# Turning the differential branch's probabilities with block transposes and DRAM

## The chip, the core and the metric

The kernel runs on one core of one Trainium2 chip. The metric is the device time of one execution in microseconds (us), as the median of a few runs. The engines are named as the profile names them: PE (TensorE, matrix products and transposes by an identity), PEld (its weight loads), DVE (VectorE), ACT (ScalarE), POOL (GpSimd) and SP (SyncE, which here only issues transfers). Each engine works through its own list of instructions in the order in which they were written down when the program was built; an instruction that has to wait holds up all that stand behind it on its engine.

## The reference

One transformer layer over 256 latent tokens and 256 context tokens, width 2048, all in float32. What bears on the change is the differential attention (branch b):

```python
def diff_attn(q, k, v, lam, lam_init, subln_g):
    b, n, h, _, dh = q.shape
    s = jnp.einsum('bnhid,bmhid->bhinm', q, k).astype(jnp.float32) * (dh ** -0.5)
    p = jax.nn.softmax(s, axis=-1)
    a = (p[:, :, 0] - lam * p[:, :, 1]).astype(v.dtype)
    o = jnp.einsum('bhnm,bmhe->bnhe', a, v)
    o = rms_norm(o, subln_g) * (1 - lam_init)
    return o.reshape(b, n, h * B_V_DIM)
```

There are 8 heads with two score maps each (head width 64, value width 128), 256 queries and 512 keys. Around it stand one large input projection, a second attention branch a (16 query heads, 4 key heads, plain softmax), two branch projections with sigmoid gates, an output projection, and a SwiGLU feed-forward part (2048 to 5632 and back).

## The kernel before

**Products.** A float32 product is made of three products of a rounded high part and a low rest (`mm3`, lines 233 to 235). A weight tile of 256 rows by 512 columns (512 KB, `wraw`) is loaded by a transfer that SP issues (L216); ACT casts its high part (`whi`, L227), DVE subtracts to get the low part (`wlo`, L229), and PE then does 12 matmuls of 128 x 512 with it. There are 7 buffers for raw weights, shared with `wada` tiles of another weight matrix that DVE sums up on the side (L431), and 3 each for `whi` and `wlo`. This stream of weights runs through the whole kernel.

**Branch b.** It is worked in 16 units (numbered 0 to 15 here), each one head and 128 queries. `front` (from L719) does the scores on PE (`s`, L740, 6 matmuls into the two `s` buffers that exist), the two softmaxes (row maximum on DVE L686, exponential on ACT L689, reciprocal L690), scales the second map (ACT L746) and combines both on DVE into one tile `p` of 128 queries by 512 keys (L747). `back` (from L752) is a generator that is resumed step by step between other pieces of work: it turns `p` with four PE transposes into a PSUM tile (`ptp`, L764), copies that to SBUF with ACT (`pT`, L770, 2 buffers), multiplies with the values (`o`, L785), takes squares on ACT (`junk_o`, L788), a power on POOL (`rstdo`, L120), scales on DVE (`on`, L790), and turns the small result with one more PE transpose (`otp`, L794).

**What sets the order.** A loop over 32 units (16 of branch b, then 16 of branch a) does `front` of a unit, resumes the older `back` generators with `on()`, and between them takes pieces of projections (`filler`, 12 big matmuls with one weight tile each) to spread the attention work evenly over the projection work. A scheduler in the language then orders each engine's list from its own estimate of when things are ready. So a change in one unit's steps also moves other instructions, on every engine.

**A turn by DRAM that is already there.** In the feed-forward part `turned` (L1038) turns a 128 x 512 tile otherwise: DVE transposes it in 32 x 32 blocks (L1041), POOL's queue writes it to DRAM (L1044), and four transfers on the same queue read it back so that the blocks change places (L1047).

## Time and profile before

| | us |
|---|---|
| median of 3 runs | 1711.54 (1708.84 to 1712.44) |
| the profiled execution | 1710.46 |
| its span in the trace | 1708.7 |
| PE busy in the span | 1682.3 |
| DVE busy | 1148.3 |
| ACT busy | 769.8 |
| POOL busy | 202.2 |
| branch b's units in the trace | about 380 to 620 |

A row of a group reads: line, engine, operation, output<-inputs, shape, count | busy us in all, mean ns of one | idle time of the engine just before them, and what ended it. A row of the timeline reads: start in us from the span's start, duration, engine, line, operation, count, and in brackets the idle time before it with what ended that. A row of a table of windows reads: window, its length, busy time of PE, PEld, DVE, ACT and POOL with counts, the granted PE clock (1.00 is full), the share of the transfer engines' time and GB/s.

### The profile page before, as it was taken

The page shows a single profiled execution, that of the slowest core. Times are in us where ns is not written, and L with a number is a line of the kernel's source. Part 1 is how long each engine was busy: PE and PEld are TensorE (multiplying, and loading weights), DVE is VectorE, ACT ScalarE, POOL GpSimd, SP SyncE. Part 2 cuts the span into 40 slices and gives each one's busy share as a digit, 9 for nine tenths or more (in the row PEclk, how much of TensorE's full clock was granted, in tenths as well). Part 3 has the DMA queues.
Part 4 walks back from the last instruction along what each step waited for, and adds up shares of the span by engine and source line. Part 5 has one row for each costly group of instructions (what it writes and reads, how often), then busy time and mean ns, then how long its engine had stood idle before and what let it go on. Part 6 is the DMA issues. An engine that isn't in the chain of part 4 may idle for free.

```text
span 1708.7 us, 21517 instructions
## 1 busy us (share of the span) xinstructions
PE 1682.3 (98%) x7889; PEld 1354.0 (79%) x7889; DVE 1148.3 (67%) x1459; ACT 769.8 (45%) x1045; POOL 202.2 (12%) x296
## 2 busy tenths in 40 slices
PE   6999999999999999999999999999999999999999
PEld 4676778887887778887888788888888888888887
DVE  5764779788788878996666755566666666554554
ACT  4222223246656556577544544444444444433332
POOL 1200002011031110001111101111111111100000
PEclk9999999999999999999999999999999999999999
DMA  7887785678757668676787857788888888765662
GB/s 285 304 295 267 265 333 175 210 259 259 251 179 220 223 224 282 231 246 206 244 272 237 295 173 222 222 271 264 266 270 265 266 275 255 237 219 191 219 205 91
DMA packets 181291, 413.15 MB, mean 242 GB/s; under 512 B 15008, under 2 KB 16240, under 8 KB 180928
## 3 DMA queue, kind: packets, MB, share of 16 engines
q1 hardware_dynamic: 168912, 374.23, 66.9%
q0 software_dynamic: 12272, 37.53, 7.2%
q8 instruction: 62, 1.02, 0.2%
q14 instruction: 45, 0.37, 0.1%
HBM read 395.42 MB, written 16.29 MB: 241 GB/s over the span
## 4 chain that ended last, share of the span: by engine, by line
PE 87%; DVE 5%; DMA 3%; ACT 2%; issue 2%; POOL 1%; SPq 0%; ACTq 0%; DVEq 0%; POOLq 0%
PE mm L233 26%; PE mm L234 26%; PE mm L235 26%; PE ada L290 2%; DVE wlo L229 1%; PE ptp L764 1%; ACT whi L227 1%; DMA wraw<-in_w_in_dram 1%; PE o L785 1%; PE s L740 1%; ACT p L689 1%; DMA fturn<-turn_d 0%; DMA tok<-in_x_dram 0%; DVE nr L479 0%; DMA gate_d<-gate 0%
## 5 line engine op out<-in xcount | busy, mean ns | idle before, releaser
L229 DVE TENSOR_TENSOR wlo<-wraw,whi 128x1024 fp32r<-128x1024 f32 x497 | 606.6, 1222 | 420.2 <-ACT whi L227 419.3
L227 ACT CAST whi<-wraw 128x1024 fp32r<-128x1024 f32 x498 | 523.0, 1051 | 729.1 <-PE mm L235 606.3
L234 PE MATMUL mm<-wlo,hT 128*128 128x512 f32 x684 | 266.2, 389 | 0.8 <-DVE wlo L229 0.8
L233 PE MATMUL mm<-whi,hT 128*128 128x512 f32 x684 | 266.2, 389 | 0.0
L235 PE MATMUL mm<-whi,hT 128*128 128x512 f32 x684 | 266.1, 389 | 0.0
L233 PE MATMUL mm<-whi,xT 128*128 128x512 f32 x630 | 251.8, 403 | 1.5 <-ACT xT L334 0.7
L234 PE MATMUL mm<-wlo,xT 128*128 128x512 f32 x630 | 247.1, 392 | 1.1 <-DVE wlo L229 1.0
L235 PE MATMUL mm<-whi,xT 128*128 128x512 f32 x630 | 246.1, 391 | 0.0
L431 DVE SCALAR_TENSOR_TENSOR ada<-wada,vt,ada 128x1024 f32<-128x1024 f32 x120 | 152.1, 1278 | 0.0
L234 PEld LDWEIGHTS mm<-wlo,hT 128*128 128x128 f32 x684 | 128.4, 188 | 27.6 <-DVE wlo L229 1.1
L233 PEld LDWEIGHTS mm<-whi,hT 128*128 128x128 f32 x684 | 128.4, 188 | 26.9 <-ACT whi L227 0.3
L235 PEld LDWEIGHTS mm<-whi,hT 128*128 128x128 f32 x684 | 128.4, 188 | 26.8
L233 PEld LDWEIGHTS mm<-whi,xT 128*128 128x128 f32 x630 | 117.7, 188 | 39.2 <-issue 13.1
L234 PEld LDWEIGHTS mm<-wlo,xT 128*128 128x128 f32 x630 | 118.5, 188 | 26.1 <-DVE wlo L229 2.9
L235 PEld LDWEIGHTS mm<-whi,xT 128*128 128x128 f32 x630 | 118.3, 188 | 25.2
L233 PE MATMUL mm<-whi,fT 128*128 128x512 f32 x354 | 137.5, 388 | 0.5 <-DVE y L1083 0.5
L234 PE MATMUL mm<-wlo,fT 128*128 128x512 f32 x354 | 137.3, 388 | 0.0
L235 PE MATMUL mm<-whi,fT 128*128 128x512 f32 x354 | 137.3, 388 | 0.0
L233 PEld LDWEIGHTS mm<-whi,fT 128*128 128x128 f32 x354 | 66.4, 188 | 15.3 <-issue 0.8
L235 PEld LDWEIGHTS mm<-whi,fT 128*128 128x128 f32 x354 | 66.4, 188 | 13.8
L234 PEld LDWEIGHTS mm<-wlo,fT 128*128 128x128 f32 x354 | 66.5, 188 | 13.5
L233 PE MATMUL mm<-whi,oT 128*128 128x512 f32 x192 | 75.9, 396 | 0.0
(241 smaller groups left out, 2153.0 us busy)
## 6 DMA issues: line engine op xcount, KB each, us to landing
wraw<-in_w_in_dram SPq DMA_DIRECT2D x159, 512.0 KB, 5.0
wada<-in_w_ada_dram SPq DMA_DIRECT2D x128, 512.0 KB, 4.7
wraw<-in_w_ff_gate_dram SPq DMA_DIRECT2D x88, 512.0 KB, 4.4
wraw<-in_w_ff_up_dram SPq DMA_DIRECT2D x88, 512.0 KB, 5.3
wraw<-in_w_ff_down_dram SPq DMA_DIRECT2D x88, 512.0 KB, 4.4
wada<-in_ada_t_dram SPq DMA_DIRECT2D x64, 512.0 KB, 5.9
wraw<-in_w_br_a_dram SPq DMA_DIRECT2D x32, 512.0 KB, 5.0
wraw<-in_w_out_dram SPq DMA_DIRECT2D x32, 512.0 KB, 5.3
```

Of the source, the lines that this page charges most:

```text
L227: last_hi.append(nc.scalar.copy(out=hi[:, 0:nk], in_=raw[:, 0:nk]))
L229: last_lo.append((by or nc.vector).tensor_tensor(out=lo[:, 0:nk], in0=raw[:, 0:nk], in1=hi[:, 0:nk].bitcast(F32), op=ALU.subtract))
L233: nc.tensor.matmul(ps, lhsT=ah, rhs=wh, start=first, stop=False, skip_group_check=skip)
L234: nc.tensor.matmul(ps, lhsT=ah, rhs=wl, start=False, stop=False, skip_group_check=skip)
L235: return nc.tensor.matmul(ps, lhsT=al, rhs=wh, start=False, stop=last, skip_group_check=skip)
L290: last_pe[0] = nc.tensor.matmul(aps[32 * g:32 * g + 32, 0:ncol], lhsT=cst[:, k, :], rhs=rhs, start=(k < 4), stop=(k >= NKT - 4))
L431: nc.vector.scalar_tensor_tensor(out=dst, in0=wt, scalar=sc[:, 0, kt:kt + 1], in1=dst, op0=ALU.mult, op1=ALU.add)
L689: nc.scalar.activation(out=p, in_=sp, func=AF.Exp, bias=mx, accum_out=rs)
L740: nc.tensor.matmul(sps[i], lhsT=qT[rows, x, hh, tk * P:(tk + 1) * P], rhs=kT["b", grp][y][rows, hh, :], start=(n == 0), stop=(n == 2))
L764: nc.tensor.transpose(out=tp[:, kt * P:(kt + 1) * P], in_=p[:, kt * P:(kt + 1) * P], identity=ident)
L785: nc.tensor.matmul(op[:, 0:BV], lhsT=pT[:, kt, :], rhs=vb[:, kt, hh * BV:(hh + 1) * BV], start=(kt == 0), stop=(kt == 3))
```

## The change

The block transpose and the transfers of `turned` become two helpers, `turn_out` (DVE transpose and POOL's write to DRAM) and `turn_in` (four reads). The feed-forward part uses them as it did its own lines, all on POOL's queue. In branch b the four PE transposes and the ACT copy of a unit go; `turn_out` is called for the unit right after its generator is made, and `turn_in`, with the four reads issued by SP, at the generator's next step. The product `o` comes one step later than that. The block-transposed tile `part` takes a buffer from the four that hold the softmax tiles `p`. Branch a keeps its PE transposes.

```diff
--- before.py
+++ after.py
@@ -680,6 +680,20 @@
         hi, lo = oT.four(g)
         split(hi, lo, o_raw(g * 4, 4).rearrange("p (k c) -> p k c", k=4))
 
+    turn_d = dram.tile([16 + 2 * (DFF // CG), P, CG], F32, name="turn_d")
+
+    def turn_out(src, n, tag="p", bufs=4):
+
+        part = scratch("part", tag=tag, bufs=bufs)
+        nc.vector.transpose(out=part, in_=src)
+        nc.gpsimd.dma_start(out=turn_d[n], in_=part)
+        return turn_d[n].rearrange("(a i) (k b j) -> b i k a j", a=4, k=4, b=4)
+
+    def turn_in(dst, blocks, by):
+
+        for b in range(4):
+            by.dma_start(out=dst[32 * b:32 * b + 32].rearrange("p k (a j) -> p k a j", a=4), in_=blocks[b])
+
     def softmax(sp):
 
         mx = small("mx", 1)
@@ -757,17 +771,17 @@
                 pair[:] = [big_tile("pT", F32R).rearrange("p (k c) -> p k c", k=4) for _ in range(2)]
             pT = list(pair)
         else:
+            blocks = turn_out(pr[0], u)
+            yield None
             pT = scratch("pT", tag="pTb", bufs=2).rearrange("p (k c) -> p k c", k=4)
-        for i, p in enumerate(pr):
+            turn_in(pT, blocks, nc.sync)
+            yield None
+        for i, p in enumerate(pr if br == "a" else []):
             tp = tp_ps("ptp")
             for kt in range(4):
                 nc.tensor.transpose(out=tp[:, kt * P:(kt + 1) * P], in_=p[:, kt * P:(kt + 1) * P], identity=ident)
-            src = tp.rearrange("p (k q) -> p k q", k=4)
-            if br == "a":
-                c0 = hh % 2 * SEQ + i * P
-                split(*[x[:, :, c0:c0 + P] for x in pT], src)
-            else:
-                nc.scalar.copy(out=pT, in_=src)
+            c0 = hh % 2 * SEQ + i * P
+            split(*[x[:, :, c0:c0 + P] for x in pT], tp.rearrange("p (k q) -> p k q", k=4))
         yield None
         if br == "a" and hh % 2 == 0:
             return
@@ -882,6 +896,8 @@
         while pieces[0] + 0.5 < goal and next(fill, fill) is not fill:
             pass
         work.append(back(br, u, pr))
+        if br == "b":
+            next(work[-1])
         if br == "a" and u % 4 == 2 and u > 4:
             o_parts(u // 4 - 1)
 
@@ -1033,19 +1049,12 @@
 
     NFT = DFF // P
     fT = Parts("fT", NFT)
-    turn_d = dram.tile([2 * (DFF // CG), P, CG], F32, name="turn_d")
-
     def turned(src, dst_hi, dst_lo, cg, tk):
 
-        part = scratch("fpart", tag="nr", bufs=2)
-        nc.vector.transpose(out=part, in_=src)
-        whole = scratch("fturn", tag="sq", bufs=2)
-        held = turn_d[2 * cg + tk]
-        nc.gpsimd.dma_start(out=held, in_=part)
-        blocks = held.rearrange("(a i) (k b j) -> b i k a j", a=4, k=4, b=4)
-        for b in range(4):
-            nc.gpsimd.dma_start(out=whole[32 * b:32 * b + 32].rearrange("p (k a j) -> p k a j", k=4, a=4), in_=blocks[b])
-        after(10 + 2 * tk, lambda: split(dst_hi, dst_lo, whole.rearrange("p (k q) -> p k q", k=4)))
+        blocks = turn_out(src, 16 + 2 * cg + tk, "nr", 2)
+        whole = scratch("fturn", tag="sq", bufs=2).rearrange("p (k q) -> p k q", k=4)
+        turn_in(whole, blocks, nc.gpsimd)
+        after(10 + 2 * tk, lambda: split(dst_hi, dst_lo, whole))
 
     for cg in range(DFF // CG):
         if cg == 2:
```

The order of the instructions around it changes with it. Three places, with the names' numbers where rows would otherwise read alike. The new lines stand 14 lines lower in this part of the file.

TensorE, from the last scores of unit 4 on. Before (`s_3587` and `s_3588` are unit 4's scores, `ptp_3611` is unit 3's turn):

```order
L740 MATMUL s_3587<-kbT0_2326,qT_2739 128x512
L740 MATMUL s_3588<-kbT0_2326,qT_2739 128x512
L764 MATMUL ptp_3611<-ident_75,p_3494 128x128 x4
L233 MATMUL mm_3405<-whi_3619,xT3_2113 128x512
L234 MATMUL mm_3405<-wlo_3620,xT3_2113 128x512
L235 MATMUL mm_3405<-whi_3619,xT3_2113 128x512
```

Now (`s_3578`, `s_3579` are unit 4's scores, `s_3693`, `s_3694` unit 5's; `pT_3513` and `on_3605` belong to unit 2, `on_3501` to unit 1):

```order
L754 MATMUL s_3578<-kbT0_2326,qT_2740 128x512
L754 MATMUL s_3579<-kbT0_2326,qT_2740 128x512
L808 MATMUL otp_3601<-ident_75,on_3501 128x128
L799 MATMUL o_3604<-vb0_106,pT_3513 128x128 x4
L754 MATMUL s_3693<-kbT0_2326,qT_2740 128x512
L754 MATMUL s_3694<-kbT0_2326,qT_2740 128x512
L754 MATMUL s_3693<-kbT0_2327,qT_2740 128x512
L754 MATMUL s_3694<-kbT0_2327,qT_2740 128x512
L808 MATMUL otp_3716<-ident_75,on_3605 128x128
L233 MATMUL mm_3408<-whi_3559,xT2_1500 128x512
```

Before, 24 big matmuls follow the scores of a unit and its predecessor's turn, and 12 more stand between a unit's `o` and the next scores; now the scores of units 4 and 5 stand next to each other, and unit 2's `otp` stands right behind unit 2's `o` and those scores, with no big matmul between.

ScalarE at the same place. Before (`junk_o_3456` is unit 1's, `p_3494` and `p_3500` unit 3's):

```order
L788 ACTIVATE junk_o_3456,sso_3457<-o_3450 128x128
L227 CAST whi_3571<-wraw_3569 128x1024
L770 COPY pT_3507<-ptp_3508 128x512
L689 ACTIVATE p_3494,rs_3495<-s_3484,mx_3492 128x512
L689 ACTIVATE p_3500,rs_3501<-s_3485,mx_3498 128x512
L227 CAST whi_3619<-wraw_3617 128x1024
L746 ACTIVATE p_3500<-p_3500,rs_3501 128x512
L227 CAST whi_3640<-wraw_3638 128x1024
```

Now (`p_3588`, `p_3594` are unit 4's, `junk_o_3610` unit 2's, `p_3703`, `p_3709` unit 5's, `junk_o_3725` unit 3's):

```order
L703 ACTIVATE p_3588,rs_3589<-s_3578,mx_3586 128x512
L703 ACTIVATE p_3594,rs_3595<-s_3579,mx_3592 128x512
L802 ACTIVATE junk_o_3610,sso_3611<-o_3604 128x128
L760 ACTIVATE p_3594<-p_3594,rs_3595 128x512
L227 CAST whi_3559<-wraw_3557 128x1024
L809 COPY o2_3498<-otp_3716 128x128
L703 ACTIVATE p_3703,rs_3704<-s_3693,mx_3701 128x512
L703 ACTIVATE p_3709,rs_3710<-s_3694,mx_3707 128x512
L760 ACTIVATE p_3709<-p_3709,rs_3710 128x512
L802 ACTIVATE junk_o_3725,sso_3726<-o_3719 128x128
L227 CAST whi_3624<-wraw_3622 128x1024
```

Before there are two or three casts of weights to a unit; now one, and it stands behind the unit's whole softmax and behind `junk_o` of an older unit.

SyncE's queue, with the semaphores that each row waits for (DMAHW: an earlier transfer of SP's, DMASW: one of POOL's). Before:

```order
L424 DMA wada_3551<-in_w_ada_dram 128x1024 [waits DVE_49]
L216 DMA wraw<-in_w_in_dram 128x2x512 [waits DMAHW3_49,DVE_49,Activation_49]
L216 DMA wraw<-in_w_in_dram 128x2x512 [waits DMAHW4_49,DMAHW2_49,DVE_49]
L424 DMA wada_3636<-in_w_ada_dram 128x1024 [waits DVE_49]
L216 DMA wraw<-in_w_in_dram 128x2x512 [waits DMAHW6_49,DVE_49]
```

Now (the first four `pT` rows are unit 2's, the last four unit 3's):

```order
L424 DMA wada_3555<-in_w_ada_dram 128x1024 [waits DMAHW0_49,DVE_49]
L695 DMA pT<-turn_d 32x16x32 [waits DMAHW1_49,DMASW6_49,PE_49]
L695 DMA pT<-turn_d 32x16x32 [waits DMAHW2_49]
L695 DMA pT<-turn_d 32x16x32 [waits DMAHW3_49]
L695 DMA pT<-turn_d 32x16x32 [waits DMAHW4_49]
L216 DMA wraw<-in_w_in_dram 128x2x512 [waits DMAHW5_49,DVE_49]
L695 DMA pT<-turn_d 32x16x32 [waits DMAHW6_49,DMAHW7_49,DMASW7_49,PE_49]
L695 DMA pT<-turn_d 32x16x32
L695 DMA pT<-turn_d 32x16x32 [waits DMAHW0_49]
L695 DMA pT<-turn_d 32x16x32 [waits DMAHW1_49]
L216 DMA wraw<-in_w_in_dram 128x2x512 [waits DMAHW2_49,DVE_49]
```

Weight loads now stand behind reads that wait for POOL's write of the same unit to have landed. Between the reads of units 2 and 3 there is one `wraw` tile, and between those of units 1 and 2 only a `wada` tile.

## Prediction

> **What bounds the kernel now.** I read the page first: busy time, then the chain that ended last.
>
> ```profile
> PE 1682.3 (98%) x7889; PEld 1354.0 (79%) x7889; DVE 1148.3 (67%) x1459; ACT 769.8 (45%) x1045; POOL 202.2 (12%) x296
> PE 87%; DVE 5%; DMA 3%; ACT 2%; issue 2%; POOL 1%; SPq 0%; ACTq 0%; DVEq 0%; POOLq 0%
> ```
>
> PE is busy for 98% of the span and is 87% of the chain. So PE work that goes is time that goes, and every us in which PE is made to wait is a us lost. The window of branch b's units decides, since everything that the change touches lies there:
>
> ```profile
> 380.00:620.00 240.00, 237.41 (x1192) 188.47 (x1190) 198.56 (x313) 143.51 (x258) 42.59 (x45) 1.00 0.71 228
> ```
>
> In these 240 us PE idles for 2.6, at full clock; DVE is 83% busy, ACT 60%, the transfers 71%. There is nothing to win here but PE work, and hardly any slack in DVE.
>
> **What goes.** Two stretches of PE's timeline, the first behind scores without a turn, the second with one:
>
> ```profile
> 382.82 0.97 PE L740 MATMUL s<-kbT,qT 64*128 64x512 f32 x6
> 384.05 0.40 PE L234 MATMUL mm<-wlo,xT 128*128 128x512 f32 x1
> 386.34 0.39 PE L235 MATMUL mm<-whi,xT 128*128 128x512 f32 x1
> ...
> 392.83 0.96 PE L740 MATMUL s<-kbT,qT 64*128 64x512 f32 x6
> 393.72 0.65 PE L764 MATMUL ptp<-ident,p 128*128 128x128 f32 x4
> 394.45 0.39 PE L234 MATMUL mm<-wlo,xT 128*128 128x512 f32 x1
> ```
>
> From the scores to the second big matmul behind them it takes 1.23 us without and 1.62 with the four transposes: 0.4 us to a unit, 16 x 0.4 = 6.4 us. The ten steps from 384.05 to 386.34 give 0.229 us for a big matmul, so 12 of one weight tile take 2.75. If the 2.6 us of idle time went as well, the gain would be 9.0; I take 6.5. The ACT copies (16 x 0.59, below) gain nothing: ACT is at 60%.
>
> ```profile
> L770 ACT COPY pT<-ptp 128x512 f32<-128x512 f32 x16 | 9.4, 588 | 4.3 <-PE ptp L764 4.3
> L1041 DVE STREAM_TRANSPOSE fpart<-act 128x512 f32<-128x512 f32 x22 | 14.3, 686 | 0.0
> L686 DVE TENSOR_REDUCE mx<-s 128x1 f32<-128x512 f32 x64 | 43.2, 682 | 5.2 <-PE s L235 4.1 <-PE s L740 0.9
> L689 ACT ACTIVATE p<-s,mx 128x512 f32<-128x512 f32 x64 | 44.1, 690 | 31.2 <-DVE mx L686 28.8 <-DVE rs L690 2.0
> L689 ACT ACTIVATION_READ_ACCUMULATOR p<-s,mx 128x1 f32 x64 | 12.7, 198 | 0.0
> L746 ACT ACTIVATE p<-p,rs 128x512 f32<-128x512 f32 x16 | 11.6, 722 | 2.7 <-DVE rs L745 2.7
> L747 DVE SCALAR_TENSOR_TENSOR p<-p,rs 128x512 f32<-128x512 f32 x16 | 12.0, 748 | 2.7 <-ACT p L746 2.7
> L120 POOL TENSOR_TENSOR rstdo<-rstdo,neghalf 128x1 f32<-128x1 f32 x16 | 16.9, 1058 | 143.3 <-DVE rstdo L119 143.3
> L227 ACT CAST whi<-wraw 128x1024 fp32r<-128x1024 f32 x496 | 521.8, 1053 | 729.1 <-PE mm L235 606.3 <-DMA wraw<-in_w_in_dram 97.4 <-issue 11.1
> L229 DVE TENSOR_TENSOR wlo<-wraw,whi 128x1024 fp32r<-128x1024 f32 x495 | 605.2, 1224 | 420.1 <-ACT whi L227 419.3
> ```
>
> **What is added, and how late it makes things.** The 16 block transposes (0.69 us each, 11 us) raise DVE to 87% of the window. By themselves they hide behind PE's matmuls; without that cover they would cost 11 us. The way from a unit's scores to its `o` is the question. From the scores to the end of `p`:
>
> ```profile
> 414.64 0.96 PE L740 MATMUL s<-kbT,qT 64*128 64x512 f32 x6
> 421.26 0.74 DVE L747 SCALAR_TENSOR_TENSOR p<-p,rs 128x512 f32<-128x512 f32 x1
> ```
>
> 415.6 to 422.0 is 6.4 us, with the transpose 7.1. Added up row by row where the lists are dense (two maxima, two exponentials, scaling, combining, transpose) it is some 6.0. Then two transfers in series, with SP's issues between:
>
> ```profile
> turn_d<-fpart POOLq DMA_DIRECT2D x22, 256.0 KB, 4.3
> fturn<-turn_d POOLq DMA_DIRECT2D x88, 64.0 KB, 6.0
> wraw<-in_w_in_dram SPq DMA_DIRECT2D x159, 512.0 KB, 5.0
> DMA to landing us min/median/max: 2.4/5.5/8.9
> wraw<-in_w_ff_gate_dram SPq DMA_DIRECT2D x5, 512.0 KB, 3.5
> 399.81 0.37 SPq L216 DMA_DIRECT2D wraw<-in_w_in_dram  x1
> 20.16 0.65 SPq L162 DMA_DIRECT2D tok_t<-in_x_t_dram  x1
> ```
>
> The write takes 4.3 us from issue to landing (bounds 2.4 and 8.9, the extremes of both kinds of `turn_d` transfer). SP's reads of this shape are not in the trace: the nearest are its plain issue, 0.37, and one with more pieces, 0.65; four of them are 1.5 to 2.6, and I take 2. So SP stands still from when it reaches a unit's reads until some 11 us after the unit's scores, and all weight loads queue behind it. A unit's `o` is due 6.5 + 4.3 + 2 + some 5 = 18 us after its scores, and the first weight tile behind the reads can be used after 6.5 + 4.3 + 2 + 0.4 + 4.6 + 1.05 (cast) = 19 us.
>
> Against that stands what PE has to do meanwhile, counted in the new order. For most units it is enough: 19 to 39 us of work stand between a unit's scores and its `o`. It is not enough at the end of each group of eight, and there the scheduler has drawn steps of attention together, which makes chains on which PE waits whatever the transfers do.
>
> **Units 2 to 5**, on the order shown in the part on the change; 0 is the end of unit 4's scores. (a) Unit 5's scores need both exponentials of unit 4, as there are two `s` buffers: a maximum and two exponentials with their read-outs, 0.68 + 2 x (0.69 + 0.20) = 2.5, with the hand-overs 2.7 us; PE has `otp` and `o` (0.8 below, from 421.62 to 422.43) for 0.9: 1.8 us of waiting. (b) Unit 2's `otp` needs `on`; this way and the length of an `o` are timed by
>
> ```profile
> 421.62 1.05 PE L785 MATMUL o<-vb,pT 128*128 128x128 f32 x8
> 422.43 0.47 PE L233 MATMUL mm<-whi,xT 128*128 128x512 f32 x1
> 422.82 0.28 ACT L788 ACTIVATE junk_o<-o 128x128 f32<-128x128 f32 x1
> 425.06 0.35 DVE L790 SCALAR_TENSOR_TENSOR on<-o,rstdo,kept 128x128 f32<-128x128 f32 x1 [0.66 <-POOL rstdo L120]
> ```
>
> 2.7 us from the end of `o` (422.7) to that of `on` (425.4). Here `junk_o` also stands behind unit 4's exponentials on ACT, so `on` is done at 4.8, while PE stands there at 3.6: 1.2. (c) The next 12 big matmuls need a weight tile whose cast stands behind `junk_o` and the scaling (3.7 to 4.8), and whose low part stands behind `on`, the combining and a maximum on DVE (6.2 to 7.4); PE has two matmuls with the high part until 5.4: 2.0. (d) The cast after that stands behind unit 3's `junk_o`, whose `o` PE ends at 11.4: 1.6. (e) Unit 7's scores need an exponential of unit 6, whose buffer is free when unit 4's write, issued at 8.1, has landed at 12.4: 0.9. (f) Units 4 and 5 have `otp` right behind `o`: 2 x 2.7. That is 12.9, taken as 13. If each of the first steps is one us shorter it is 9; if the write in (e) takes 8.9 and the reads of unit 3 are a little late as well, 19.
>
> **Units 8 to 15** are spread better. Unit 14's scores stand right behind unit 13's: 1 us. Behind unit 13's reads the first new weight tile is used after 12.8 us of PE work (36 big matmuls, 12 for scores, two `o`), 13.8 with that wait, and is there after 19: 5 more. With 2.4 for the write, 3.5 for the weights and 6.0 for the dense softmax it would be 1 more; with 8.9 for the write and 7.1 before it, and the weights a us later behind the reads' own data, 12. So 6, bounds 2 and 13. Nothing is charged for the rest: in the feed-forward part the same transfers stay on the same queue, and branch a keeps its way.
>
> The Trainium skill has a smaller price for a transfer ("DMA: Bandwidth & Descriptors", section on the anatomy of one DMA): about 2.0 us fixed plus the bytes by 436 GB/s, so by estimate 2.6 for the write and 3.2 for a weight tile. With these unit 13 would cost 2 us instead of 5, and the time would come out 3 lower; the rows above, from a chip with other transfers under way, say 4.3 and 4.6 to 5.0, and I stay with them.
>
> **Sum** for the profiled execution, 1710.46 (1.1 below the median of the runs, 1711.54): 13 + 6 of new waiting less 6.5 of PE work, +12.5, **1723 us**. Bounds: 9 + 2 - 9 gives +2, 1712; 19 + 13 - 6.5 gives +25.5, 1736.
>
> **Rivals.** *The waits are hidden and the transposes saved* (faster): 1710.5 - 6.5 = 1704. For it: PE's share of the chain, and 19 or more us of cover for most units. Against it: (b) and (f) hold no transfer at all and PE has nothing else listed there. 8%. *Waits about as large as the gain*: transfers land at their shortest and (a) to (e) overlap more than I count, so 13 + 6 becomes 6 to 9: 1710 to 1714. 12%. *The clock falls too* (slower than forecast). This happens at the kernel's start when PE is kept waiting:
>
> ```profile
> 18.00:22.00 4.00, 2.08 (x8) 1.05 (x7) 3.49 (x4) 2.55 (x8) 2.02 (x1) 1.00 1.05 387
> 22.00:26.00 4.00, 1.79 (x4) 1.31 (x5) 2.68 (x10) 2.36 (x7) 0.55 (x1) 0.56 1.05 384
> 26.13 0.63 PE L371 MATMUL mm<-wlo,xT 128*128 128x512 f32 x1
> 26.56 0.63 PE L370 MATMUL mm<-whi,xT 128*128 128x512 f32 x1
> ```
>
> After some 3 us of waiting PE's granted clock is 0.56, and a matmul comes every 0.43 us instead of 0.23; twelve such matmuls lose 2.4 us. Two such falls in each group, from the point where single waits reach about 3 us, with late writes besides (+17 to +22 before it): 1732 to 1742. 18%. The Trainium skill ("TensorE: Matmul & The Clock Gate", Part 1) says that the clock halves after an idle window of about 3.4 us; by that rule (a) to (d), broken by short work, would not trigger it, and unit 13's 5 us would.
>
> **Numbers.** Forecast 62%: 1723, own range 1715 to 1732. The 8 in 10 range leaves out the faster rival and the tail of the clock's: 1711 to 1740. About 0.2% (3.4 us) is what a measurement of this kernel can tell from no change: faster 0.08, same 0.10, slower 0.82.
>
> **What would show it.** In the changed kernel's window from 380 on, PE's idle time rises from 2.6 to about 22 us, in two clusters, at units 2 to 5 and 13; PE's matmuls `otp` wait for DVE `on`, and `s` for ACT's exponentials; some `wraw` casts wait for SP's loads instead of PE. The block transposes take 0.69 us and 16 of them appear; the four reads take SP 1.5 to 2.6 us to issue. The prediction fails if PE's idle time there stays below 7 us, or if most units wait for their reads, which would mean that the reads land later than 8 us after their issue and the loss is nearer 40.

## The result, and the profile after

The changed kernel takes 1747.87 us (median of 5 runs, 1744.27 to 1751.35) against 1709.9 (5 runs, 1708.84 to 1712.44): ratio 1.0224, 95% interval 1.0213 to 1.0235. It is 2.2% slower, 38 us. The profiled execution took 1751.35, with a span of 1749.6; the one of before 1710.46 and 1708.7. So there are 40.9 us to explain.

The page of the changed kernel, busy times and PE's granted clock in 40 slices of the span (tenths of full speed, 9 is 90% or more):

```profile
PE 1700.2 (97%) x7825; PEld 1361.5 (78%) x7825; DVE 1156.5 (66%) x1475; ACT 761.1 (43%) x1029; POOL 204.9 (12%) x312
PEclk9999999999899889999999999999999999999999
```

PE does 64 instructions less and is busy 17.9 us longer (1682.3 before). With the 6.4 us of transposes that are gone, the work that is left became 24 us slower. The rest is idle time: 1749.6 - 1700.2 = 49.4 us against 26.4 before, +23. So 23 + 24 - 6.4 = 41: **waiting and a lower clock share the loss about evenly.** The ends of matmuls are modelled, so the parts are rough: the clock's part is 24 us by this count and 19 by the one below. The stretch of branch b's units before, and then by stage after (columns: PE, PEld, DVE, ACT, POOL busy with their counts, PE's clock, DMA share, GB/s):

```profile
380.00:660.00 280.00, 276.03 (x1375) 220.30 (x1374) 234.32 (x365) 168.47 (x299) 45.50 (x47) 1.00 0.72 229
```

```profile
380.00:520.00 140.00, 122.63 (x533) 92.98 (x532) 102.44 (x164) 64.64 (x117) 28.72 (x33) 0.94 0.72 217
520.00:580.00 60.00, 60.00 (x295) 47.74 (x294) 47.63 (x78) 35.36 (x63) 7.03 (x13) 1.00 0.67 198
580.00:660.00 80.00, 68.68 (x276) 50.78 (x275) 54.58 (x85) 32.67 (x61) 9.66 (x14) 0.87 0.78 241
```

All of it lies in the two groups of branch b's units: 17.4 us idle in the first, 11.3 in the second, none between; before, 4.0 in the whole stretch. The clock's part by this view is 0.06 x 140 + 0.13 x 80 = 19 us. What PE waits for between 380 and 660 (us in total, times, longest), and what SP waits for there:

```profile
PE mm L234 <- DVE wlo L229: 7.8, 9, 1.1
PE mm L233 <- ACT whi L227: 7.8, 7, 1.6
PE otp L808 <- DVE on L804: 7.1, 4, 3.1
PE o L799 <- DMA pT<-turn_d: 1.9, 1, 1.9
```

```profile
SPq L695 <- DMA turn_d<-part: 56.3, 11, 8.4
```

The waits are short and many. The largest share stands at the big matmuls, for both parts of the weights, 15.6 us where it was 1.0 before; only one `o` waited for its reads. SP's row is new: 56 us in which SP stood at a read until POOL's write had landed. What that means is seen best in SP's own timeline, before and after, over the same 25 us (start, us, line, what, count; `wada` rows left out):

```profile
403.49 3.72 SPq L216 DMA_DIRECT2D wraw<-in_w_in_dram  x2
...
410.65 3.04 SPq L216 DMA_DIRECT2D wraw<-in_w_in_dram  x2
...
417.08 4.65 SPq L216 DMA_DIRECT2D wraw<-in_w_in_dram  x2
...
424.36 3.82 SPq L216 DMA_DIRECT2D wraw<-in_w_in_dram  x2
```

```profile
401.10 0.89 SPq L216 DMA_DIRECT2D wraw<-in_w_in_dram  x2
410.20 3.48 SPq L695 DMA_DIRECT2D pT<-turn_d  x4
...
414.47 2.68 SPq L695 DMA_DIRECT2D pT<-turn_d  x4
417.24 0.84 SPq L216 DMA_DIRECT2D wraw<-in_w_in_dram  x1
424.38 2.60 SPq L695 DMA_DIRECT2D pT<-turn_d  x4
427.07 0.57 SPq L216 DMA_DIRECT2D wraw<-in_w_in_dram  x1
```

Before, two weight tiles are issued every 7 us. After, one tile is issued between 402 and 427: the reads of units 1, 2 and 3 stand close together in the queue, and SP issues nothing for 8 us before the first of them and for 6 before the last. A weight tile lasts PE 2.75 us, so 25 us of matmuls need nine.

That the tiles land late is not the whole of it. The one tile of this stretch, issued at 417.24, had landed 4.4 us later, and its cast ran at 428:

```profile
424.95 0.27 ACT L809 COPY o<-otp 128x128 f32<-128x128 f32 x1 [5.30 <-PE otp L808]
...
427.39 0.72 ACT L760 ACTIVATE p<-p,rs 128x512 f32<-128x512 f32 x1 [0.23 <-DVE rstdo L119]
428.02 1.03 ACT L227 CAST whi<-wraw 128x1024 fp32r<-128x1024 f32 x1
```

The cast stands behind unit 4's whole softmax in ACT's list, and ACT was idle for 5.3 us ahead of that. Between 380 and 660 the casts of the changed kernel waited 5.9 us in all for tiles. So here PE waits for weights mostly because their casts stand late in ACT's list; why the list is so is the question of the experiments.

### The profile page after: what moved, and what is told of

Same layout as the page of the kernel before. It is cut to its first block, busy times and chain, and to the rows that moved or that the text cites. A ratio compares the mean times of both kernels' runs of the same rounds, so it can differ in the third digit from the quotient of the medians.

```text
span 1749.6 us, 21538 instructions
## 1 busy us (share of the span) xinstructions
PE 1700.2 (97%) x7825; PEld 1361.5 (78%) x7825; DVE 1156.5 (66%) x1475; ACT 761.1 (43%) x1029; POOL 204.9 (12%) x312
## 4 chain that ended last, share of the span: by engine, by line
PE 62%; DVE 3%; DMA 2%; issue 2%; ACT 1%; POOL 0%; DVEq 0%; ACTq 0%; POOLq 0%; SPq 0%
PE mm L234 20%; PE mm L235 20%; PE mm L233 19%; DMA wraw<-in_w_in_dram 1%; DVE wlo L229 1%; PE ptp L782 1%; DMA gate_d<-gate 0%; ACT p L703 0%; ACT whi L227 0%; PE o L233 0%; DMA x_d<-xn 0%; PE o L235 0%; PE o L234 0%; DVE ada L431 0%; PE s L235 0%
## 5 line engine op out<-in xcount | busy, mean ns | idle before, releaser
L234 PE MATMUL mm<-wlo,xT 128*128 128x512 f32 x630 | 254.4, 404 | 7.9 <-DVE wlo L229 7.8
L233 PE MATMUL mm<-whi,xT 128*128 128x512 f32 x630 | 253.1, 409 | 8.8 <-ACT whi L227 7.8
L235 PE MATMUL mm<-whi,xT 128*128 128x512 f32 x630 | 251.5, 399 | 0.0
L233 PEld LDWEIGHTS mm<-whi,xT 128*128 128x128 f32 x630 | 119.9, 193 | 51.4 <-issue 14.0
L234 PEld LDWEIGHTS mm<-wlo,xT 128*128 128x128 f32 x630 | 122.2, 194 | 39.5 <-DVE wlo L229 13.6
L235 PEld LDWEIGHTS mm<-whi,xT 128*128 128x128 f32 x630 | 121.9, 193 | 25.8
```

Source lines behind the costliest of these rows:

```text
L233: nc.tensor.matmul(ps, lhsT=ah, rhs=wh, start=first, stop=False, skip_group_check=skip)
L234: nc.tensor.matmul(ps, lhsT=ah, rhs=wl, start=False, stop=False, skip_group_check=skip)
L235: return nc.tensor.matmul(ps, lhsT=al, rhs=wh, start=False, stop=last, skip_group_check=skip)
```

## Experiments

Three theories were set against each other: **O**, the scheduler drew the attention steps together and PE waits on chains of ACT and DVE; **L**, the detour through DRAM is too long for `o`; **T**, weight loads stand behind SP's wait for POOL's write. T fell in its plain form and came back as **S**: what counts is where the reads stand in SP's list.

All ratios are against the kernel before on the same chip (medians 1708.3 to 1708.8 there).

| run | us | ratio (95% interval) |
|---|---|---|
| reads on POOL's queue | 1717.17 | 1.0049 (1.0037 to 1.0062) |
| order of PE held | 1742.26 | 1.0197 (1.0181 to 1.0213) |
| reads don't wait for the write | 1721.67 | one run |
| PE's order of before drawn together | 1708.82 | 0.9999 (0.9990 to 1.0008) |
| a small waiting read on SP | 1711.62 | 1.0015 (1.0006 to 1.0025) |
| the same on POOL | 1711.02 | 1.0015 (1.0006 to 1.0024) |
| reads on POOL, `o` later | 1716.56 | 1.0043 (1.0030 to 1.0056) |
| reads on SP later | 1736.81 | 1.0163 (1.0150 to 1.0177) |
| unused reads on SP | 1745.24 | 1.0213 (1.0198 to 1.0229) |
| unused reads on POOL | 1720.33 | 1.0062 (1.0049 to 1.0074) |
| one plain read | 1707.48 | 0.9997 (0.9988 to 1.0005) |
| one plain read, `o` later | 1705.78 | 0.9984 (0.9975 to 0.9993) |
| four plain reads | 1706.64 | 0.9992 (0.9983 to 1.0000) |
| four plain reads, `o` later | 1707.34 | 0.9993 (0.9984 to 1.0001) |
| lead taken | 1742.87 | 1.0207 (1.0191 to 1.0223) |
| lead halved | 1724.30 | 1.0097 (1.0083 to 1.0111) |

### Is it the order, the wait or the way?

*The reads on POOL's queue.*

```diff
-            turn_in(pT, blocks, nc.sync)
+            turn_in(pT, blocks, nc.gpsimd)
```

> The four reads of a unit go to POOL's queue, as in the feed-forward part; the block transposes, POOL's write and the later `o` stay. The order of PE's list is spread again: 36 to 48 big matmuls between the scores of two units, where the changed kernel has 0, 12 and 2 at units 4 to 7. If the loss comes from the order (theory O: the scheduler's list draws attention steps together, PE waits for chains on ACT and DVE, and its clock falls): the 6.5 us of saved PE work show, 1703 to 1707, PE idle below 6 us between 380 and 640, clock 1.00. If the loss comes from the detour by DRAM itself being too long for a unit's `o` (theory L): still over 1725, with PE waiting for the reads. If it comes from weight loads that stand behind SP's waits (theory T): also 1703 to 1710, as SP is free again; T and O are told apart by the next run.

1717.17. Most of the loss goes, but not the last 8 us. PE's waits there are led by

```profile
PE o L799 <- DMA pT<-turn_d: 8.0, 5, 4.2
```

which fits L for this remainder. In this run the scheduler also spread PE's list again, so it does not tell O from T by itself.

*PE's order held*: scores, `o` and `otp` may not be placed ahead of the big matmuls that come before them in the program; reads on SP as in the change.

```diff
+            with tc.issue_after(last_mm[0].ins):
                 nc.tensor.matmul(sps[i], ...)
...
+            with tc.issue_after(last_mm[0].ins):
                 nc.tensor.matmul(op[:, 0:BV], ...)
...
+        with tc.issue_after(last_mm[0].ins):
             nc.tensor.transpose(out=tp[:, 0:P], in_=on, identity=ident)
```

> The changed kernel with its reads on SP, but each unit's scores, `o` and `otp` are held behind the last big matmul that stands before them in the program, so PE's list is spread as in the kernel before (36 to 48 big matmuls between scores). SP still waits for POOL's write ahead of the reads, with weight loads behind. Theory O: the waits go with the order, 1703 to 1712, clock 1.00. Theory T (SP's waits make the weights late): PE now waits for casts and these for weight loads, 20 us or more of idle time stay, over 1730.

1742.26: 5.6 us won of 38. With the order spread, the waits moved. PE, ACT and SP between 380 and 660:

```profile
PE mm L233 <- ACT whi L227: 17.5, 8, 3.1
PE mm L234 <- DVE wlo L229: 6.4, 9, 1.3
```

```profile
ACT whi L227 <- DMA wraw<-in_w_in_dram: 26.2, 14, 7.5
```

```profile
SPq L697 <- DMA turn_d<-part: 83.0, 16, 8.1
```

The chain is in plain sight here: SP stands before all 16 units' reads, the casts wait for tiles that are loaded late (26.2 us, against 5.9 in the changed kernel), PE waits for the casts. The number of big matmuls between the scores of any two units is that of the kernel before, and PE waits neither for `on` nor for exponentials; the loss is nearly as large. So it doesn't need the drawn-together order.

*Reads that don't wait for the write.* They read another tensor of the kernel, so the probabilities don't enter `o` in this run.

```diff
-            blocks = turn_out(pr[0], u)
+            turn_out(pr[0], u)
+            blocks = t["rows"][0].rearrange(...)
```

> The four reads on SP read a constant input of the same shape in DRAM instead of the tile that POOL has just written, so SP waits for no write of POOL's (POOL still writes; the probabilities that `o` uses are left out). Same number, size and issue cost of transfers. The list is spread in the first four units and drawn together at units 4 to 7 (two scores with 2 and 0 big matmuls between). Theory T: no waits of SP, so 1703 to 1707. Theory O: the remaining bunch costs part of it, 1706 to 1720. If the issue time of SP's reads (4 x 0.63 us per unit) or their traffic were the cause, it would stay above 1735.

1721.67, in a single run: 26 us of the 38 go with the wait. The list of SP is no better than the changed kernel's: at most 3 weight loads from later in the program stand ahead of a unit's reads, and none at eleven of the 16 units. PE's list is drawn together in two places only, with 14 and 0 big matmuls between the scores of units 5 and 6, 13 and 14. SP still stood at the reads, 38.5 us until PE's `o` had freed the tile that they fill. What makes the 13 us that stay was not separated.

*The kernel before, drawn together*: its PE transposes, its loads, but 2, 0, 1 and 0 pieces of filling work after units 3 to 6.

```diff
-        take(fill, 2)
+        near = {3: 2, 4: 0, 5: 1, 6: 0}.get(n)
+        take(fill, 2 if near is None else near)
```

> The kernel before (PE transposes, no detour by DRAM at all) with its program order changed at units 3 to 6 alone: 2, 0, 1 and 0 pieces of projection follow these units instead of three to four each, and the pieces left out follow later. PE's list then has the scores of units 4 to 8 drawn together, with `otp` close behind `o`, as the changed kernel has. Theory O: slower by 8 to 25 us, 1718 to 1735, with PE idle in one cluster near 430 to 470 and a fall of the granted clock there. Theory T or L: within 3 us of the kernel before, as no transfer is added.

1708.82, and PE idles for 1.6 us between 380 and 620:

```profile
380.00:620.00 240.00, 238.42 (x1189) 188.66 (x1189) 204.46 (x337) 148.44 (x272) 46.02 (x45) 1.00 0.68 218
```

There are 4, 8 and 10 big matmuls between the scores of units 4 to 7, where the change has 0, 12 and 2. Attention steps so close together cost nothing while weights are there: theory O, by which the order alone costs, falls.

### The wait by itself

The kernel before, PE's order as it was but for the last unit, plus block transposes, writes, and on SP's queue one read of 128 x 8 that waits for the unit's write and that nobody uses; then the same read on POOL's queue.

```diff
+            turn_out(pr[0], u)
+            yield None
+            seen = scratch("seen", 8, tag="seen", bufs=1)
+            nc.sync.dma_start(out=seen, in_=turn_d[u][:, 0:8])     # second run: nc.gpsimd
```

> This is the kernel before, with its transposes and copies as they were and PE's order as it was. Added are the 16 block transposes on VectorE, the writes on GpSimd's queue, and on SP's queue, where the changed kernel has its four reads, one small read (128 x 8) that waits for the unit's write and that nobody uses. So nothing of `o` hangs on the detour; only SP stands still. Theory T (the weight loads stand behind SP's wait for the write): most of the loss is here, 1725 to 1745, with PE's big matmuls waiting for whi and wlo and ACT's casts for wraw. Theory L (the detour is too long for `o`) and an effect of the added DVE work: 1708 to 1712, PE idle as before.

> As the run with the wait alone, but the small read that waits for the write is on GpSimd's queue instead of SP's; all else is the same, PE's order too. Theory T: back to the time before, 1708 to 1712, since no weight stands behind the wait. If the added transposes, writes or transfers cost by themselves (DVE or the DMA engines as the bound): as high as the run with the read on SP, or at least 1715.

1711.62 and 1711.02: no difference, and T as I had put it fails. SP did stand before all 16 reads:

```profile
SPq L777 <- DMA turn_d<-part: 43.5, 16, 4.2
```

```profile
380.00:660.00 280.00, 275.14 (x1371) 219.51 (x1370) 242.34 (x380) 167.61 (x298) 53.23 (x63) 1.00 0.74 243
```

44 us of standing, at full clock, with PE idle for 4.9. The added DVE work and writes cost 2.5 us by themselves (0.15%). What differs from the run with the order held is the longest stand, 4.2 against 8.1 us. SP's list shows why: the number behind a tile's name grows in program order, so it can be counted how many weight loads (`wraw`) from later in the program stand ahead of a unit's read. I call this the **lead**, for units 0 to 15:

| kernel | lead at each unit's reads | us |
|---|---|---|
| the change | 6 5 2 0 0 0 0 0, 8 6 4 3 2 0 0 0 | 1747.87 |
| PE's order held | 6 5 2 0 4 2 1 1, 8 6 4 3 2 0 5 0 | 1742.26 |
| reads on SP later | 4 3 0 0 0 0 0 0, 5 4 2 1 0 0 0 0 | 1736.81 |
| small waiting read | 6 7 6 6 6 5 7 7, 8 6 5 6 5 5 5 1 | 1711.62 |

With a lead of six tiles, 6 x 2.75 = 16 us of PE's work have been issued beyond the place of the read when SP comes to a stand; with none, nothing has. Two more runs bear on the way to `o`. One step of the filling work more before the reads on SP, or behind the reads on POOL:

```diff
+            yield None
             turn_in(pT, blocks, nc.sync)
```

> The changed kernel with its reads still on SP, but issued one step of the filling work (12 to 24 big matmuls, 2.8 to 5.5 us) later, and `o` later by as much. Theory T: SP finds the write landed or nearly so and its queue stands still for some 4 us less at each unit, so a half or more of the loss goes: 1712 to 1728. If the loss lay in the reads landing too late for `o` (L), it stays, since the reads are issued later too: 1740 to 1750.

1736.81: 11 us better, less than T gave it. The scheduler had used the freedom to draw its lists together as before.

```diff
             turn_in(pT, blocks, nc.gpsimd)
             yield None
+            yield None
```

> The reads on GpSimd's queue (as in the run at 1717), and `o` one step of the filling work later, which puts 24 big matmuls instead of none or 4 between the next unit's scores and `o`: about 5.5 us more cover for the detour. In the run at 1717 `o` waited 8.0 us for its reads. If that is the whole remainder (theory L, for what is left): these waits fall below 2 us and the transposes saved show, 1702 to 1709. If the remainder comes from the fuller queues or the clock: 1714 to 1718.

1716.56. PE's first wait there is now

```profile
PE o L800 <- DMA pT<-turn_d: 4.8, 2, 3.3
```

so `o`'s waits fell from 8.0 to 4.8 us, not below 2, and the time moved by 0.6 only: these waits are at most a part of the remainder of the runs on POOL's queue.

### The reads by themselves, and reads without small pieces

*The whole detour beside the kernel before*: all four reads of a unit, back into the tile that was written, used by nobody. `o` still gets its probabilities from PE.

```diff
+            blocks = turn_out(pr[0], u)
+            yield None
+            turn_in(blocks[1], blocks[0], nc.sync)     # second run: nc.gpsimd
```

> The kernel before with its transposes and copies, and beside them the whole detour: block transposes, writes, and all four reads of a unit on SP's queue, back into the tile that was written, where nobody uses them. Nothing of `o` hangs on it. In the list that the scheduler makes for SP, the reads of units 3 to 6 stand behind 2, 1, 0 and 0 weight loads from later in the program, where a single small read stood behind 4 to 7: the loads have lost their lead, and PE's list is drawn together again. Theory S (the four reads make the scheduler's list, the lost lead makes PE wait for weights): most of the loss comes back, 1730 to 1755. Theory L (`o` waits for its reads): 1708 to 1713.

> As the run with the unused reads, but all four on GpSimd's queue; PE's order is that of the kernel before and SP has no wait. Theory S: 1709 to 1713, as with the single small read. If the transfers themselves (fuller DMA engines, weights landing later) cost what was left in the run with the reads on GpSimd's queue: 1715 to 1720.

1745.24 on SP: **nearly the whole loss, though no `o` hangs on the reads**; only the buffer that they fill comes free later. The lead is 6 5 2 1 0 0 0 0, 0 6 5 5 3 2 2 0. PE is busy for 1700.6 us, as long as in the changed kernel, and its waits between 380 and 660 are led by those for weights, 8.7 us for `whi` and 3.7 for `wlo`.

On POOL it is 1720.33, just above the range of the second theory (the transfers themselves cost) and far outside that of S. POOL's own work stands behind the reads there. POOL's group of the reads (busy, mean ns, idle before and releasers), and DVE's waits for POOL's `rstdo` between 380 and 660:

```profile
L696 POOL DMA_DIRECT2D part<-turn_d x64 | 47.3, 823 | 64.6 <-DMA turn_d<-part 28.3 <-issue 11.7 <-PE mm L235 8.3
```

```profile
DVE on L808 <- POOL rstdo L120: 9.5, 12, 2.9
```

An issue of such a read takes POOL 0.82 us, and the longest wait of `on` for POOL is 2.9 us. What makes the 8 to 12 us of the runs on POOL's queue, these waits or the transfers themselves, stays open.

*One plain read.* POOL writes a unit in four transfers already in the turned order; SP reads the tile in one plain transfer.

```diff
-            blocks = turn_out(pr[0], u)
+            part = scratch("part", tag="p", bufs=4)
+            nc.vector.transpose(out=part, in_=pr[0])
+            whole = turn_d[u].rearrange("(b i) (k a j) -> a i k b j", b=4, k=4, a=4)
+            for x in range(4):
+                nc.gpsimd.dma_start(out=whole[x], in_=part[32 * x:32 * x + 32].rearrange("p (k b j) -> p k b j", k=4, b=4))
...
-            turn_in(pT, blocks, nc.sync)
+            nc.sync.dma_start(out=pT, in_=turn_d[u].rearrange("p (k c) -> p k c", k=4))
```

> The change with the pieces of 128 bytes moved from the read to the write: GpSimd's queue writes a unit in four transfers already in the turned order, and SP reads it with one plain transfer, still waiting for the write. In the list the reads stand behind 3 to 8 later weight loads again, and PE's list is spread as with the reads on GpSimd's queue, with none to 9 big matmuls between the next scores and `o`. Theory S: the waits for weights go and the clock stays full; what is left is `o` waiting for its reads, so 1705 to 1717. If SP's wait for the write as such is what costs: 1735 to 1748.

> As the run with one read, and `o` one step of the filling work later (24 big matmuls, 5.5 us, between the next scores and `o`). Theory S with hidden latency: the saved transposes show, 1702 to 1708, faster than before. If something else than the waits for `o` keeps the gain down, as in the run with the reads on GpSimd's queue and a later `o` (1716.6): 1711 to 1718.

1707.48, and with `o` a step later 1705.78, 0.16% (0.07 to 0.25) faster than before: the lowest time of all kernels here. The lead is 8 8 7 7 7 6 9 9, 8 8 7 7 7 6 6 3. SP still waits for the write and PE no longer for weights; SP's, PE's waits and the whole stretch with one read, and `o` not later:

```profile
SPq L781 <- DMA turn_d<-part: 21.2, 16, 4.5
```

```profile
PE o L803 <- DMA pT<-turn_d: 6.2, 3, 3.3
PE mm L234 <- DVE wlo L229: 0.3, 1, 0.3
```

```profile
380.00:660.00 280.00, 273.53 (x1322) 217.75 (x1321) 244.91 (x380) 163.26 (x285) 86.82 (x112) 0.99 0.80 262
```

With `o` later, the first of these waits is gone.

### The lead taken away

Still open was whether the list does it, or the reads' number or pieces on the chip. *Four plain reads* (32 rows of 2 KB each) instead of one; *the lead taken* and *halved* in the run with one read, whose transfers stay as they are.

```diff
-            nc.sync.dma_start(out=pT, ...)
+            for x in range(4):
+                nc.sync.dma_start(out=pT[32 * x:32 * x + 32], ...)
```

> As the run with one read, but the plain read is cut into four again (32 partitions of 2 KB rows each), so SP issues four reads to a unit and waits as in the change; only the pieces of 128 bytes are on the write's side. The list keeps the lead: 6 to 9 later weight loads ahead of each read, and 5 to 19 big matmuls stand between the next scores and most `o`. Theory S (the lead in the list decides): 1703 to 1708. If the number of issues or waits on SP costs: 1715 or more.

> As the run with four plain reads, and `o` one step of the filling work later. Theory S: 1702 to 1706, the lead kept and the reads covered; a rest of up to 4 us against the 1702 that the saved transposes would give stands for POOL's and the DMA engines' added work. If the later `o` costs by itself: 1708 to 1712.

1706.64 and 1707.34, with a lead of 5 to 10 for all units but the last. Four reads cost no more than one. The later `o` gives nothing more here, so the 0.16% of the run before is the best of sixteen kernels and small, not a gain to count on.

```diff
+        with tc.issue_after(last_read[0].ins) if last_read else nullcontext():
             nc.sync.dma_start(out=raw[:, 0:nk], ...)
...
-            nc.sync.dma_start(out=pT, ...)
+            last_read[:] = [nc.sync.dma_start(out=pT, ...)]
+            # halved: last_read[:] = last_read[-1:] + [nc.sync.dma_start(out=pT, ...)]
```

> The run with one read, whose transfers cost nothing to speak of, with its weight loads pinned in the list behind the read before them: no weight load from later in the program stands ahead of a unit's read any more (lead 0 for all 16 units, where it was 6 to 9). The transfers are untouched. Theory S: the loss comes back, 1730 to 1760, with PE waiting for whi and wlo and the clock below full. If the pieces of 128 bytes in SP's reads are what costs on the chip: it stays at 1705 to 1712.

> As the run with the lead taken, but each load is pinned behind the read before the last: lead 0 or 1 for the first four units, 3 to 6 for the others. Theory S, by dose: the first four units lose as before and the others nearly nothing, 1712 to 1730. A theory without the lead: 1705 to 1712.

Lead 0 for all units: 1742.87. Lead 0 0 0 1 4 3 4 6, 3 3 3 3 3 3 6 3: 1724.30. Both times lie where theory S had them. The edit moves nothing but the place of the weight loads, and 35 us came back without any read in small pieces on SP. But more than the lead changed by it. The scheduler, left to itself, now drew PE's list together: the scores of units 1 to 4 stand next to each other with 2 big matmuls among them, those of units 5 to 7 with none. And SP, with no load to issue ahead of a read, stood 151.5 us where it had stood 21.2. The run with the lead taken, between 380 and 660:

```profile
380.00:660.00 280.00, 260.77 (x1148) 201.71 (x1147) 214.61 (x335) 140.19 (x251) 85.71 (x108) 0.91 0.69 232
```

```profile
SPq L784 <- DMA turn_d<-part: 151.5, 27, 27.3
```

```profile
PE s L757 <- ACT p L706: 8.8, 8, 2.5
```

```profile
ACT whi L230 <- DMA wraw<-in_w_in_dram: 20.7, 12, 4.0
```

PE's busy time is that of the changed kernel again (1700.4 us in the page), and the clock is 0.91 instead of 0.99. The casts wait for tiles, as expected; PE itself waits mostly for exponentials of scores that stand too close (8.8 us) and only 3.6 us for weights, which the expectation had otherwise. Standing as such is not what costs: the run with the lead halved stood 148.0 us and lost 16, and in its second group (580 to 660), with 3 to 6 loads ahead of each read, PE ran at full clock with 2.0 us idle.

So the loss takes two ways, and they were not priced apart: weights come late, and the scheduler's lists, made with late loads, put attention steps next to each other and casts behind them. Both begin at one place. With the loads ahead of the reads, SP's waits cost nothing (1705.8 to 1711.6 in five runs), and neither does a drawn-together order (1708.82); with few loads or none ahead of many of the reads, the time is 1737 to 1748 in five runs, be PE's order held as before, `o` free of the reads, or the read a plain one. **The lost lead is the cause**; the lists show where it came from: the scheduler keeps the lead for one small read, for one plain read and for four plain reads of 64 KB, and gives it up for four reads in pieces of 128 bytes on SP, also where they wait for no write. On the chip a read of the latter kind landed in 3.0 us (median, row below), not later than a plain one of the same size in the run with four plain reads:

```profile
pT<-turn_d SPq DMA_DIRECT2D x64, 64.0 KB, 3.7
```

That it is the scheduler's estimate for such pieces which moves the list is the reading that fits; its estimates were not looked into.

## Why the prediction was wrong

The direction was right. The 1723 was 25 us too low against the median and 28 against the profiled execution, for which it was made; its range ended at 1732, the wider one at 1740.

**Right.** PE bounds the stage and 64 PE instructions go (7889 to 7825). The pieces of the detour were near: block transpose 0.71 us (0.69 forecast), the write 4.4 (4.3), four issues on SP 4 x 0.63 = 2.5 (bounds 1.5 to 2.6). From the changed kernel, the transpose's group, the transfers between 380 and 660 (KB each, median us to landing), and the reads (ns, minimum, median, maximum):

```profile
L688 DVE STREAM_TRANSPOSE part<-p 128x512 f32<-128x512 f32 x16 | 11.3, 708 | 0.3
```

```profile
turn_d<-part POOLq DMA_DIRECT2D x16, 256.0 KB, 4.4
pT<-turn_d SPq DMA_DIRECT2D x64, 64.0 KB, 3.0
```

```profile
L695 SPq DMA_DIRECT2D pT<-turn_d x64: 563/628/2421, 397.6 to 634.6; - x64
```

Only the landing of the reads was taken too long, 5 us for 3.0, and `o` hardly ever waited for them. That "SP stands still from when it reaches a unit's reads until some 11 us after the unit's scores, and all weight loads queue behind it" is what SP's timeline shows, and the idle time did come in two clusters. The smaller price for a transfer that the prediction took from the Trainium skill ("DMA: Bandwidth & Descriptors", Anatomy of one DMA), 2.6 us for the write, was rightly set aside: the trace has 4.4. That section gives its fit for transfers of POOL's queue, so it says nothing of a weight tile, which SP issues.

**The step that failed, first: what makes PE wait in units 2 to 5, and how long.** I wrote that there "the scheduler has drawn steps of attention together, which makes chains on which PE waits whatever the transfers do", and priced the chains (a) to (f) one by one, 13 us. The chains exist and are shorter, as in PE's timeline behind unit 4's scores:

```profile
426.29 0.50 PE L754 MATMUL s<-kbT,qT 64*128 64x512 f32 x1 [0.49 <-ACT p L703]
426.96 0.97 PE L754 MATMUL s<-kbT,qT 64*128 64x512 f32 x5 [0.17 <-ACT p L703]
428.52 0.33 PE L808 MATMUL otp<-ident,on 128*128 128x128 f32 x1 [0.59 <-DVE on L804]
429.10 0.73 PE L233 MATMUL mm<-whi,xT 128*128 128x512 f32 x2 [0.26 <-ACT whi L227]
...
430.91 0.79 PE L234 MATMUL mm<-wlo,xT 128*128 128x512 f32 x1 [1.07 <-DVE wlo L229]
```

(a) measured 0.7 instead of 1.8, (b) 0.6 instead of 1.2, (c) 1.3 instead of 2.0; further on (d) took 1.4 instead of 1.6, the two of (f) 1.7 each instead of 2.7, and (e) did not show. That is 7.3 us of the 12.9. The other 10 of the 17.4 us idle in this group stand at places that the sum had at nothing, at casts and low parts of later weight tiles above all; that 13 came near the total is luck.

What failed is "whatever the transfers do". Drawing steps together costs nothing while the loads keep their place (1708.82), and holding them apart leaves 34 of the 38 us when they don't (1742.26). In the run with the lead taken only loads were moved, and the lists drew together. The place of the loads should have been a term of the sum: I counted the time behind a single read for unit 13 and not how many loads stand between one read and the next. In my own quotation of SP's queue there is one weight tile between the reads of units 2 and 3, and none between those of 1 and 2; at 2.75 us to a tile that row pointed at the result. In the second group the 6 us for late weights stand against 11.3 measured with what else is idle there.

**Second: the clock.** The sum had nothing for it. It was a rival at 18% with +4.8 us to a group, "from the point where single waits reach about 3 us". It fell with shorter ones. Windows of 2 us, and PE's timeline:

```profile
412.00:414.00 2.00, 2.00 (x12) 1.16 (x11) 2.00 (x3) 0.27 (x1) 0.42 (x1) 1.00 0.54 153
414.00:416.00 2.00, 0.94 (x5) 0.44 (x3) 1.20 (x3) 1.45 (x4) 0.00 (x0) 1.00 0.83 117
416.00:418.00 2.00, 1.11 (x7) 1.14 (x8) 0.32 (x2) 0.00 (x0) 0.00 (x0) 0.82 1.01 292
418.00:420.00 2.00, 2.00 (x7) 1.69 (x7) 0.24 (x2) 0.98 (x3) 0.57 (x1) 0.50 0.96 167
```

```profile
416.89 1.68 PE L799 MATMUL o<-vb,pT 128*128 128x128 f32 x8 [1.95 <-DMA pT<-turn_d]
...
418.80 0.63 PE L234 MATMUL mm<-wlo,xT 128*128 128x512 f32 x1
```

One wait of 1.95 us, and the clock is at 0.50 a microsecond after it ends, with PE already working. The Trainium skill ("TensorE: Matmul & The Clock Gate", Part 1) gives an idle window of about 3.4 us and says that the window runs freely, without regard to when work starts; taken as a rule that only a silence of that length throttles, as I had weighed it, it is contradicted by this row, and the measurement decides. In the whole stretch the clock cost 19 us by the windows and 24 by PE's busy time, and it is the larger part of the error: idle time was forecast at about 22 us and measured 28.7.

**What would have made it wrong** was named half: most units waiting for their reads, with a loss near 40. The loss came near 40 while only one unit waited for its reads.

**The gain** of 6.4 us is there, but most of it is spent: the added DVE work and writes take 2.5 us (the small waiting reads), and of the 3.9 left 2.7 were had in the fastest version. In the change itself none of it shows.

## What to carry to other kernels

When a transfer that must wait is put on a queue that also feeds the bounding engine, count in that queue's list how many loads from later in the program stand ahead of each wait, and set their worth in work of the bounding engine against the length of the stand: here a lead of five to eight tiles (one at the last unit) hid 44 us of standing, in 16 stands of at most 4.2 us, and a lead of none cost 35. Where a scheduler makes the lists, a change can move that lead and, with it, the order on every other engine; so read its list for the queue before the list of the engine that waits. In this kernel the clock had to be charged for broken waits of 2 us, not only for long silences.

## What the runs showed of the hardware

A wait in SP's queue holds everything behind it: 402 to 410 in the timeline above without one issue. The Trainium skill ("DMA: Bandwidth & Descriptors", Anatomy of one DMA) says that a semaphore wait takes place on the issuing sequencer, before the transfer is handed over; the trace agrees, with 56.3 us of such standing. A read of 64 KB in pieces of 128 bytes took SP 0.63 us to issue and landed in 3.0; plain, it landed in 3.7, so the small pieces did not make SP's reads land later. POOL takes 0.82 us for such an issue. And the clock at 0.50 after one wait of 1.95 us had not been expected. How much of the loss the clock would take if PE were kept busy through the waits was not tried.
